# A hand-ordered head: two scan parts interleaved otherwise, states issued among the lag kernels, lag kernels in two column parts

## The chip, the cores and the metric

The kernel runs on one core of a Trainium2 chip. The metric is the device time of one execution in microseconds (us), the median of several runs. Before the change it is 1875.63 us (three runs, 1875.13 to 1880.0).

## The reference

One layer of a trunk: RMSNorm, an S5 mixer with a GLU, residual, RMSNorm, a gated convolutional FFN, residual, RMSNorm. There are 512 prompt tokens and 8 sample rows, D = 2048, D_FF = 5632; the S5 has 128 groups of 16 channels with 64 complex states each.

```python
def _s5_mixer(u, h_re, h_im, lam_re, lam_im, log_dt, b_re, b_im, c_re, c_im, d, w_glu):
    ...
    bu_re = jnp.einsum('gnp,btgp->btgn', bb_re, ug)
    bu_im = jnp.einsum('gnp,btgp->btgn', bb_im, ug)
    ...
    _, _, hs_re, hs_im = lax.associative_scan(combine, (a_re, a_im, bu_re, bu_im), axis=1)
    y = jnp.einsum('gpn,btgn->btgp', c_re, hs_re) - jnp.einsum('gpn,btgn->btgp', c_im, hs_im)
    y = y.reshape(bsz, t, D_MODEL) + d * uf
    z = jax.nn.gelu(y)
    out = z * jax.nn.sigmoid(z @ w_glu)
    return out, hs_re[:, -1], hs_im[:, -1]
...
    u = xn @ w_up ; gate = xn @ w_gate
    c = sum(full[:, j:j + t] * w_conv[j] for j in range(CONV_W)) + b_conv
    out = (jax.nn.gelu(c) * gate) @ w_down
```

## The kernel before

The program has two halves. The first, `s5_phase`, makes z, the input of the GLU. The second is dense matrix work on TensorE (L1182 for the GLU and the down projection, L1363 for the up and gate projections), each product of float32 taken as three products of high and low parts. It begins with the first matmul of L1182, which needs z of octet 0 and the first split weight.

In `s5_phase` the 128 groups are handled in eight octets (0 to 7). The prompt is cut into 64 chunks of 8 tokens. In each octet the work is: chunk inputs (C), then a scan over the chunks that carries the complex state, then from the state at each chunk's start its share in the outputs (F, L956), added on VectorE (O, L968) to the part that comes from inside the chunk (I, L827), transposed and passed through GELU (G, L977 and L980), and split into a high and a low part (Z). The part from inside the chunk is a matmul with a lag matrix; that one is made by `lag_kernel` (L, lines 887 to 893 on TensorE, a copy on ScalarE, a DMA to DRAM and one back). The tables for it are made by VectorE and GpSimd (tA, tB, tC).

The scan has two parts: "a" is octets 0 to 3, "b" octets 4 to 7, each with its own products (`sc0`, `sc1`) and sums (`wk0`, `wk1`). A chunk step of a part is three VectorE instructions, of which each needs the one before:

```python
            if k == 0:
                V.tensor_tensor(prod, v[:, :, None, :].to_broadcast([128, 2, 2, v.shape[2]]), tab, op=OP.mult)
            elif k == 1:
                V.tensor_tensor(w, vn, prod[:, 0], op=OP.add)
            else:
                V.tensor_tensor(vn, w, prod[:, 1], op=OP.add)
```

These are lines 219 (x), 221 (y) and 223 (z). A step is 128 partitions by 128 elements in x, by 64 in y and z.

What sets the order of work on every engine is a text, ORDER, written out by hand. `run` reads it from left to right. A token is a name and letters, as `a50x:D` (step 50 of the a part, instruction x, on VectorE): each name is a generator, and each letter lets it do its next stage. A, D, G stand for ScalarE, VectorE and GpSimd, Q for a DMA, a digit is a bank of PSUM, and `=w1s3` picks buffers. Each engine keeps the order in which its instructions are issued, and waits are made by data alone, so a token's place counts against the others of its engine.

At the start, ORDER holds the squares of the prompt rows (SQ), the row scales (RS: a matmul of L327, then the steps of `rsqrt_steps`, L104 to L115, on VectorE with one ScalarE root), the eight scaled rows (N, L146 or ScalarE), the transposes that make u (U, L345), and the products for the chunk inputs (mA, mB, mC on VectorE L674 and GpSimd L138).

Before, the two parts go step by step together from a14x on, the b part somewhat behind. The states F of octets 0 to 3 stand behind all eight lag kernels. F of octets 4 to 7 stands behind the b part's last instruction; then come G, Z and the split of the first weight (WT).

Of the kernel before, what the change touches and what calls it, by code (L numbers as in the profile page):

```python
# [59 lines left out]
a19x:D tC1.1:D =c0 cs2:G a19y:D tB1.1:D tB1.0:G SO1:Q a19z:D L0:A b5x:D a20x:D IB1:A b5y:D tC1.1:G a20y:D b5z:D a20z:D  # L60
b6x:D a21x:D b6y:D a21y:D b6z:D a21z:D =w0s6 tA2.0:G b7x:D a22x:D tB2.0:D SO0:Q =y1 SY0:1 a22y:D tB1.0:G b7y:D a22z:D
tB2.0:D a23x:D b7z:D =w1 tA2.1:G a23y:D b8x:D a23z:D tC2.1:D a24x:D tB2.1:G b8y:D =c0 cs4:D a24y:D b8z:D a24z:D b9x:D
a25x:D L1:0 b9y:D tC2.1:G SY0:A a25y:D tB2.1:D b9z:D a25z:D b10x:D =w1s2 tA3.0:G a26x:D tB3.0:D a26y:D b10y:D a26z:D
tC3.0:G b10z:D a27x:D b11x:D =m0 L0:Q a27y:D b11y:D a27z:D b11z:D SY1:3 a28x:D tB3.0:G IB2:A b12x:D tC3.0:D L1:A
# [25 lines left out]
I7:A I7:A GS3:A =y0 O4.0:D G3.0:0 F4.1:3 G3.0:A O4.1:D G3.1:2 G3.1:A =s2 Z3:A SF:G Z3:D F5.0:1 GS4:A =y1 O5.0:D G4.0:0  # L90
G4.0:A F5.1:3 O5.1:D G4.1:2 G4.1:A =s1 Z4:A Z4:D F6.0:1 GS5:A =y0 O6.0:D G5.0:0 G5.0:A F6.1:3 O6.1:D G5.1:2 G5.1:A =s0
Z5:A Z5:D F7.0:1 GS6:A =y1 O7.0:D G6.0:0 G6.0:A F7.1:3 O7.1:D SF:2 SF:A G6.1:1 G6.1:A =s7 Z6:D Z6:D GS7:A G7.0:0
G7.0:A G7.1:3 G7.1:A =s5 Z7:AD
# [1767 lines left out]
```

## Time and profile before

| | us |
|---|---|
| median of 3 runs | 1875.63 |
| profiled execution | 1877.71 |
| its span | 1875.9 |
| mean granted TensorE clock | 0.984 |
| TensorE busy | 1792.9 (96%) |
| VectorE busy | 1218.7 (65%) |
| ScalarE busy | 770.7 (41%) |
| GpSimd busy | 163.7 (9%) |

Engines in the rows: PE is TensorE's matmuls, PEld its weight loads, DVE VectorE, ACT ScalarE, POOL GpSimd. The shares are averages over two very different halves: the page's slices show VectorE and GpSimd full in the head and TensorE full behind it. A row of a timeline stands for one instruction or some of the same kind in a row (xN); its second number is from the first one's start to the last one's end. The end of a matmul is modelled.

### The profile page before, as it was taken

How to read it: one execution, taken by the hardware profiler on the slowest of the kernel's cores; microseconds unless marked ns; L12 is line 12 of the kernel's file. 1: busy time of each engine (PE TensorE's matmuls, PEld its weight loads, DVE VectorE, ACT ScalarE, POOL GpSimd, SP SyncE). 2: the span in 40 equal slices, each digit the busy share in tenths (PEclk: the TensorE clock that was granted, in tenths of full speed). 3: DMA queues.
4: the chain of work that ended last, by engine and by line, in shares of the span. 5: the costliest groups of instructions: out<-in, count | busy, mean ns of one | idle time of the engine just before them, and what ended most of it. 6: DMA issues, size and time to landing. Idle time of an engine off the chain costs nothing.

```text
span 1875.9 us, 36773 instructions
## 1 busy us (share of the span) xinstructions
PE 1792.9 (96%) x15962; PEld 1764.7 (94%) x15962; DVE 1218.7 (65%) x1812; ACT 770.7 (41%) x1103; POOL 163.7 (9%) x167
## 2 busy tenths in 40 slices
PE   3889999999699999999999999999999999999996
PEld 2778899999699999999999999999999999999996
DVE  8999633347887887887887887887733434343344
ACT  5763423344455454455445455544421212121223
POOL 4787201110000000000000000000000000000000
PEclk9989999999799999999999999999999999999998
DMA  7544254432434544443544534443663434333313
GB/s 148 118 136 145 72 161 141 136 125 102 146 124 147 190 136 169 169 147 124 185 165 144 194 125 147 152 133 124 221 214 94 144 98 138 103 124 118 113 68 92
DMA packets 217133, 259.43 MB, mean 138 GB/s; under 512 B 33859, under 2 KB 190491, under 8 KB 215867
## 3 DMA queue, kind: packets, MB, share of 16 engines
q1 hardware_dynamic: 213938, 252.17, 41.5%
q10 hardware_dynamic: 2842, 4.88, 0.9%
q8 instruction: 125, 2.05, 0.5%
q14 instruction: 36, 0.29, 0.1%
q0 software_dynamic: 192, 0.03, 0.0%
HBM read 226.11 MB, written 60.49 MB: 153 GB/s over the span
## 4 chain that ended last, share of the span: by engine, by line
PE 87%; DVE 6%; DMA 2%; ACT 2%; issue 1%; POOL 0%; SPq 0%; ACTq 0%; DVEq 0%; POOLq 0%
PE bank L1363 44%; PE bank L1182 35%; PE bank L1787 2%; PE py L956 1%; DMA x<-in_x_prompt_dram 1%; PE pv L698 1%; DVE m L138 1%; PE pm L683 1%; PE pk L893 1%; DVE op L1455 0%; DVE b L1442 0%; PE pu L345 0%; PE bank L1681 0%; DMA braw<-in_s_b_im_dram 0%; PE pt L977 0%
## 5 line engine op out<-in xcount | busy, mean ns | idle before, releaser
L1363 PE MATMUL bank<-op,w 128*128 128x260 f32 x5040 | 618.7, 284 | 9.0 <-DVE w L1337 5.2
L1363 PEld LDWEIGHTS bank<-op,w 128*128 128x128 f32 x5040 | 613.1, 189 | 10.6 <-DVE w L1337 5.7
L1182 PE MATMUL bank<-act,wh 128*128 128x260 f32 x2496 | 400.0, 282 | 0.0
L1182 PEld LDWEIGHTS bank<-act,wh 128*128 128x128 f32 x2496 | 341.3, 188 | 0.0
L1328 ACT ACTIVATE w<-raw 128x1024 fp32r<-128x1024 f32 x252 | 266.0, 1056 | 168.6 <-PE bank L1363 86.1
L1337 DVE TENSOR_TENSOR w<-raw,w 128x1024 fp32r<-128x1024 f32 x252 | 305.6, 1219 | 24.4 <-ACT w L1328 23.3
L1141 ACT ACTIVATE wh<-raw 128x2048 fp32r<-128x2048 f32 x61 | 116.8, 1916 | 464.5 <-PE bank L1182 462.7
L1363 PE MATMUL bank<-fz,w 128*128 128x260 f32 x2016 | 251.1, 284 | 5.1 <-DVE w L1337 4.8
L1363 PEld LDWEIGHTS bank<-fz,w 128*128 128x128 f32 x2016 | 246.7, 190 | 5.7 <-DVE w L1337 5.0
L1182 PE MATMUL bank<-act,wl 128*128 128x260 f32 x1248 | 250.9, 282 | 0.0
L1145 DVE TENSOR_TENSOR wl<-raw,wh 128x2048 fp32r<-128x2048 f32 x60 | 137.5, 2292 | 163.0 <-ACT wh L1141 163.0
L1182 PE MATMUL bank<-z,wh 128*128 128x260 f32 x1280 | 207.4, 284 | 3.2 <-DVE cps L1278 2.9
L1182 PEld LDWEIGHTS bank<-act,wl 128*128 128x128 f32 x1248 | 192.1, 188 | 0.0
L1182 PEld LDWEIGHTS bank<-z,wh 128*128 128x128 f32 x1280 | 176.4, 189 | 4.1 <-issue 3.3
L1182 PE MATMUL bank<-z,wl 128*128 128x260 f32 x640 | 129.0, 283 | 0.0
L1763 DVE TENSOR_TENSOR h<-h,bank 128x260 f32<-128x260 f32 x80 | 29.6, 421 | 130.9 <-PE bank L1182 130.9
L1763 DVE TENSOR_TENSOR uh<-uh,bank 128x260 f32<-128x260 f32 x80 | 29.6, 421 | 115.1 <-PE bank L1182 115.1
L1182 PEld LDWEIGHTS bank<-z,wl 128*128 128x128 f32 x640 | 98.9, 189 | 0.0
L1328 ACT ACTIVATE w<-s 128x1024 fp32r<-128x1024 f32 x42 | 44.6, 1062 | 74.8 <-PE bank L1363 73.1
L1586 DVE TENSOR_TENSOR us<-us,bank 128x260 f32<-128x260 f32 x21 | 8.9, 424 | 69.5 <-PE bank L1363 69.5
L1344 DVE TENSOR_TENSOR raw<-raw 128x1024 f32<-128x1024 f32 x42 | 51.4, 1225 | 1.4
L1341 DVE TENSOR_TENSOR raw<-raw,s 128x1024 f32<-128x1024 f32 x42 | 51.4, 1225 | 1.4
(351 smaller groups left out, 1811.3 us busy)
## 6 DMA issues: line engine op xcount, KB each, us to landing
raw<-in_ffn_w_down_dram SPq DMA_DIRECT2D x44, 1024.0 KB, 5.8
raw<-in_ffn_w_up_dram SPq DMA_DIRECT2D x42, 1024.0 KB, 5.1
raw<-in_ffn_w_gate_dram SPq DMA_DIRECT2D x42, 1024.0 KB, 6.8
raw<-in_s_w_glu_dram SPq DMA_DIRECT2D x16, 1024.0 KB, 6.2
a_dram<-cv SPq DMA_DIRECT2D x44, 260.0 KB, 2.1
src<-a_dram SPq DMA_DIRECT2D x11, 1040.0 KB, 8.1
x<-in_x_prompt_dram SPq DMA_DIRECT2D x16, 512.0 KB, 9.2
m<-kd SPq DMA_DIRECT2D x32, 256.0 KB, 4.5
```

Source lines behind the costliest of these rows:

```text
L138: engine[e].tensor_tensor(dst, a, b, op=op)
L683: PE.transpose(pm[:, e * 128:(e + 1) * 128], bps[o, eh][0][:, ri, e].rearrange("p q s -> p (q s)"), ident)
L1141: A.activation(hi, raw, AF.Copy)
L1145: engine[e].tensor_tensor(lo, raw, hi.bitcast(F32), op=OP.subtract)
L1182: PE.matmul(ps[hf][:, 0:HALF], w, x[:, hf * HALF:(hf + 1) * HALF], start=first and i < 2, stop=last and i >= 4)
L1328: A.activation(w[:, 0], u.q[name], AF.Copy)
L1337: V.tensor_tensor(w[:, 1], u.q[name], w[:, 0].bitcast(F32), op=OP.subtract)
L1341: V.tensor_tensor(u.q["A22"], u.q["A22"], u.q["S3"], op=OP.subtract)
L1344: V.tensor_tensor(u.q["A12"], u.q["A12"], u.q["S2"], op=OP.subtract)
L1363: PE.matmul(bank, w[:, a, kk], x[:, kk], start=name in BEGINS and kk + i == 0, stop=kk == 7 and i == 2, skip_group_check=True)
L1763: V.tensor_tensor(t, t, x, op=OP.add)
L1787: PE.matmul(ps, w[:, kk, ni * 128:(ni + 1) * 128], x[:, kk, c0:c1], start=kk + i == 0, stop=kk == 3 and i == 2)
```

## The change

The order text is rewritten in two stretches. In its head, the row scales RS come earlier, with no GpSimd operation issued next to them; scaled row N7 goes to GpSimd, N3 and N4 to ScalarE, the other five to VectorE (before: four each on ScalarE and VectorE); the clearing for the sample rows (SM) comes later. In the scan, from step 14 of the a part on, three a instructions stand for each b instruction, so the a part is ahead of the b part; F, O and G of octets 0 to 3 and the first high parts (Z) stand among the lag kernels and the rest of the b part; the low parts of octets 0 to 2 stand on VectorE behind the b part's end, where before two of them were on GpSimd.

`lag_kernel` issues its matmuls so that neighbours write the two halves of the output partitions (0 to 31, 32 to 63) in turn. Eight matmuls with the identity become two, with a summing matrix `stack` and a spread-out `dge`, which four ScalarE copies make; `stack` and `quarter` come from two more VectorE reductions. Four of the eight loads of x are issued on ScalarE's queue.

```diff
--- before.py
+++ after.py
@@ -25,10 +25,10 @@
...
-mB1.0:D mC1.0:G =b1p1 mA1.1:D AL:A RS:1 mC1.1:D mB1.0:G mP1.0.1:2 RS:D XU:D mB1.1:D RS:A XU:A RS:D mB1.1:G mP1.0.1:A
+=b1p1 mA1.1:D RS:D RS:A RS:D mB1.0:G N4:A N1:D N7:G DG0:A AL:A N5:D N2:D mP1.0.1:2 mP1.0.0:3 mC1.1:D N0:D N3:A XU:D
...
@@ -53,44 +53,44 @@
...
-a50x:D b32x:D tC6.1:G a50y:D b32y:D tB6.1:D a50z:D b32z:D YM:G a51x:D L6:1 b33x:D I3:A =c1 cs7:G a51y:D b33y:D a51z:D
...
+b13x:D a51x:D a51y:D a51z:D b13y:D tC5.0:G a52x:D a52y:D L4:3 =w0 tA5.1:D a52z:D b13z:D tB5.1:G a53x:D a53y:D a53z:D
...
@@ -189,6 +189,8 @@
         s5 = ctx.enter_context(tc.tile_pool(name="s5", bufs=1))
         vs = s5.tile([128, 73, 2, 64], F32, name="vs")
         dgm = s5.tile([128, 16, 16], F32, name="dgm")
+        stack = s5.tile([128, 32], F32, name="stack")
+        quarter = s5.tile([128, 4], F32, name="quarter")
         ysm = s5.tile([128, 2, 8, 8], F32, name="ysm")
         a1 = s5.tile([128, 2, 64], F32, name="a1")
         at3 = s5.tile([128, 3, 8, 64], F32, name="at3")
@@ -257,15 +259,15 @@
             nc.sync.dma_start(xs8, x_sample[:, 0, :])
             nc.sync.dma_start(xsr, dram(x_sample, 0, [[128, 128], [1, 128]]))
 
-            def load_x(i, where):
+            def load_x(i, where, second=nc.sync):
 
                 x = slot([128, 2, 1024], F32, "x", where)
                 for g2 in range(2):
-                    nc.sync.dma_start(x[g2 * 64:g2 * 64 + 64],
+                    (nc.sync, second)[g2].dma_start(x[g2 * 64:g2 * 64 + 64],
                                       dram(x_prompt, 2 * i * D + g2 * 1024, [[8 * D, 64], [D, 2], [1, 1024]]))
                 return x
 
-            xt = [load_x(i, i + 1) for i in range(4)]
+            xt = [load_x(i, i + 1, nc.scalar) for i in range(4)]
             for i, src_ in ((0, s5_d), (1, norm_mix)):
                 for g2 in range(2):
                     nc.gpsimd.dma_start(dld[:, i].rearrange("p (a g q) -> p a g q", a=4, g=2)[:, :, g2, :],
@@ -310,6 +312,8 @@
             dgc = s5t.tile([128, 2, 16], F32, name="dgc")
             mq = s5t.tile([128, 16], F32, name="mq")
             V.tensor_reduce(mq, ident.rearrange("p (a b) -> p b a", b=16), axis=AX.X, op=OP.add)
+            V.tensor_reduce(stack, ident.rearrange("p (a b) -> p b a", b=32), axis=AX.X, op=OP.add)
+            V.tensor_reduce(quarter, ident.rearrange("p (a b) -> p a b", b=32), axis=AX.X, op=OP.add)
             sel = s5t.tile([128, NB], F32, name="sel")
             V.tensor_reduce(sel, ident.rearrange("p (a b) -> p a b", b=16), axis=AX.X, op=OP.add)
 
@@ -840,6 +844,10 @@
         ysz = s5y.tile([128, 2, 8, 8], F32, name="ysz")
         for g2 in range(2):
             P.memset(bk[g2 * 64:g2 * 64 + 64, :, :, (1 - g2) * 16:(1 - g2) * 16 + 16], 0.0)
+
+        dge = s5y.tile([128, 16, 4, 16], F32, name="dge")
+        for e in range(4):
+            A.activation(dge[:, :, e], dgm, AF.Copy, scale=quarter[:, e:e + 1])
         m3s = {}
         css = {}
         w3 = {}
@@ -881,17 +889,23 @@
             kt = kts[o % 2]
             pk = pst("pk", (yield))
             m3 = m3s[o]
-            for e in range(8):
-                rows = slice((e // 4) * 32, (e // 4) * 32 + 32)
-                c0 = (e % 4) * 128
-                PE.matmul(pk[rows, c0:c0 + 16], ident[:, (e % 4) * 32:(e % 4) * 32 + 32], dgm[:, 2 * o + e // 4, :],
+            half = [slice(eh * 32, eh * 32 + 32) for eh in range(2)]
+            for eh in range(2):
+                PE.matmul(pk[half[eh]].rearrange("p (e k) -> p e k", e=4)[:, :, 0:16], stack, dge[:, 2 * o + eh],
                           start=True, stop=False)
+            for e4 in range(4):
+                c0 = e4 * 128
                 for ri in range(2):
-                    PE.matmul(pk[rows, c0:c0 + 16], bk[:, ri, e, :], ct[:, ri, o * 8 + e, :],
-                              start=False, stop=ri == 1)
+                    for eh in range(2):
+                        PE.matmul(pk[half[eh], c0:c0 + 16], bk[:, ri, eh * 4 + e4, :], ct[:, ri, o * 8 + eh * 4 + e4, :],
+                                  start=False, stop=e4 == 3 and ri == 1)
+            for e4 in range(4):
+                c0 = e4 * 128
                 for ri in range(2):
-                    PE.matmul(pk[rows, c0 + 16:c0 + 128], bk[:, ri, e, :],
-                              m3[:, ri, e, 0:7].rearrange("p k q -> p (k q)"), start=ri == 0, stop=ri == 1)
+                    for eh in range(2):
+                        PE.matmul(pk[half[eh], c0 + 16:c0 + 128], bk[:, ri, eh * 4 + e4, :],
+                                  m3[:, ri, eh * 4 + e4, 0:7].rearrange("p k q -> p (k q)"),
+                                  start=ri == 0, stop=ri == 1)
             yield
             copy("A", kt.rearrange("p l e q -> p e l q"),
                  pk[0:64].rearrange("p (e l q) -> p e l q", e=4, l=8))
```

VectorE, in the middle of the scan (sc_100 and wk_102 belong to the a part, sc_101 and wk_103 to the b part), before:

```order
L219 TENSOR_TENSOR sc_100<-vs,sc_100 128x128
L219 TENSOR_TENSOR sc_101<-vs,sc_101 128x128
L221 TENSOR_TENSOR wk_102<-vs,sc_100 128x64
L221 TENSOR_TENSOR wk_103<-vs,sc_101 128x64
L223 TENSOR_TENSOR vs<-wk_102,sc_100 128x2x32
L223 TENSOR_TENSOR vs<-wk_103,sc_101 128x2x32
```

The same place after (now sc_102 and wk_104 belong to the a part, sc_103 and wk_105 to the b part, and the lines are 221, 223 and 225):

```order
L221 TENSOR_TENSOR sc_103<-vs,sc_103 128x128
L221 TENSOR_TENSOR sc_102<-vs,sc_102 128x128
L223 TENSOR_TENSOR wk_104<-vs,sc_102 128x64
L225 TENSOR_TENSOR vs<-wk_104,sc_102 128x2x32
L223 TENSOR_TENSOR wk_105<-vs,sc_103 128x64
L221 TENSOR_TENSOR sc_102<-vs,sc_102 128x128
L223 TENSOR_TENSOR wk_104<-vs,sc_102 128x64
L225 TENSOR_TENSOR vs<-wk_104,sc_102 128x2x32
L225 TENSOR_TENSOR vs<-wk_105,sc_103 128x2x32
```

Before, an instruction of one part always stands between two that depend on each other; now x, y and z of the a part follow each other directly, with one b instruction after each z.

TensorE, where the states of octet 0 come (m_0 is octet 0's table, m_7 octet 7's), before:

```order
L887 MATMUL pk<-dgm,ident 32x16
L890 MATMUL pk<-ct,bk 32x16 x2
L893 MATMUL pk<-m_7_2375,bk 32x112 x2
L956 MATMUL py<-m_0_1411,vs 64x128 x32
L956 MATMUL py<-m_1_1487,vs 64x128 x16
L977 MATMUL pt<-ident,ys 128x128 x4
```

The same place after (lag kernels are lines 894 to 906, the intra part 831, the states 970, the transposes 991):

```order
L831 MATMUL py_2263<-m_2173,uz 64x128 x8
L831 MATMUL py_2272<-m_2173,uz 64x128 x8
L970 MATMUL py<-m_0_1420,vs 64x128 x32
L894 MATMUL pk<-dge,stack 32x4x16 x2
L900 MATMUL pk<-ct,bk 32x16 x16
L906 MATMUL pk<-m_6_2178,bk 32x112 x16
L991 MATMUL pt<-ident,ys 128x128 x4
L970 MATMUL py<-m_1_1496,vs 64x128 x16
```

The states of octet 0 stood behind the lag kernel of octet 7; now they stand ahead of that of octet 6.

## Rows read from the trace of the kernel before

**Rows 1.** The page: span.
```profile
span 1875.9 us, 36773 instructions
```

**Rows 2.** Stages: PE, PEld, DVE, ACT, POOL busy (count), PEclk, DMA share, GB/s.
```profile
90.25:181.10 90.85, 79.28 (x1361) 71.83 (x1360) 89.84 (x377) 46.34 (x87) 76.60 (x68) 0.89 0.48 145
181.10:205.83 24.73, 24.73 (x372) 22.64 (x372) 17.80 (x63) 8.83 (x15) 4.81 (x2) 0.97 0.34 94
...
231.49:1875.90 1644.41, 1609.43 (x13325) 1603.93 (x13325) 1017.49 (x1177) 644.72 (x883) 23.57 (x34) 0.99 0.42 140
```

**Rows 3.** DVE timeline, a part alone: start, length, instruction, count, [idle before].
```profile
104.41 0.30 DVE L219 TENSOR_TENSOR sc<-vs,sc 128x128 f32<-128x128 f32 x1
104.74 0.22 DVE L221 TENSOR_TENSOR wk<-vs,sc 128x64 f32<-128x64 f32 x1
104.99 0.22 DVE L223 TENSOR_TENSOR vs<-wk,sc 128x64 f32<-128x64 f32 x1
105.25 0.30 DVE L219 TENSOR_TENSOR sc<-vs,sc 128x128 f32<-128x128 f32 x1
```

**Rows 4.** DVE timeline, both parts interleaved.
```profile
176.51 0.48 DVE L219 TENSOR_TENSOR sc<-vs,sc 128x128 f32<-128x128 f32 x2
176.91 0.34 DVE L221 TENSOR_TENSOR wk<-vs,sc 128x64 f32<-128x64 f32 x2
177.17 0.34 DVE L223 TENSOR_TENSOR vs<-wk,sc 128x64 f32<-128x64 f32 x2
177.43 0.48 DVE L219 TENSOR_TENSOR sc<-vs,sc 128x128 f32<-128x128 f32 x2
```

**Rows 5.** DVE timeline, b part alone: two x in turn.
```profile
198.67 0.30 DVE L219 TENSOR_TENSOR sc<-vs,sc 128x128 f32<-128x128 f32 x1
...
199.51 0.30 DVE L219 TENSOR_TENSOR sc<-vs,sc 128x128 f32<-128x128 f32 x1
```

**Rows 6.** DVE timeline, last rows of the a part and the b part.
```profile
180.85 0.34 DVE L223 TENSOR_TENSOR vs<-wk,sc 128x64 f32<-128x64 f32 x2
...
205.62 0.21 DVE L223 TENSOR_TENSOR vs<-wk,sc 128x64 f32<-128x64 f32 x1
```

**Rows 7.** DVE waits from 181.1 to 206: total, times, longest us.
```profile
DVE ys L968 <- PE py L956: 5.3, 4, 3.4
```

**Rows 8.** TensorE in a window: PE busy (count), PEclk, DMA share, GB/s.
```profile
176.00:178.00 2.00, 1.83 (x14) 0.50 0.32 80
```

**Rows 9.** PE timeline of the tail.
```profile
207.31 2.08 PE L956 MATMUL py<-m,vs 64*64 64x128 f32 x32
209.32 0.66 PE L977 MATMUL pt<-ident,ys 128*128 128x128 f32 x4
209.91 2.07 PE L956 MATMUL py<-m,vs 64*64 64x128 f32 x32
...
214.28 2.08 PE L956 MATMUL py<-m,vs 64*64 64x128 f32 x32 [1.72 <-DVE ys L968]
...
231.49 0.74 PE L1182 MATMUL bank<-z,wh 128*128 128x260 f32 x4 [0.25 <-ACT uz L980]
```

**Rows 10.** Head: timelines of DVE, PE and POOL, and one window as in rows 2.
```profile
35.00 0.17 DVE L104 TENSOR_SCALAR rq<-prs 128x8 f32<-128x8 f32 x1 [2.86 <-PE prs L327]
...
35.97 2.44 DVE L111 TENSOR_TENSOR rq<-rq,rs 128x8 f32<-128x8 f32 x2
...
39.13 0.64 DVE L115 TENSOR_TENSOR rs<-rs,rq 128x8 f32<-128x8 f32 x1
...
47.13 2.03 DVE L146 TENSOR_SCALAR vs<-x,rs 128x1024 f32<-128x1024 f32 x1
...
49.31 2.79 PE L345 MATMUL pu<-ident,vs 128*128 128x128 f32 x12 [1.22 <-DVE vs L146]
...
35.90 2.48 POOL L138 TENSOR_TENSOR bp<-bb,bp 128x512 f32<-128x512 f32 x2 [2.97 <-DVE bp L674]
...
30.00:32.00 2.00, 0.00 (x0) 0.00 (x0) 2.00 (x4) 0.01 (x1) 1.57 (x2) 1.00 1.07 229
```

More of the change, by code (lines that the diff above doesn't have):

```diff
@@ L27 @@
 ORDER = """
-=s5 SM:A SQ1:A SQ0:A SQ2:A SQ3:A SQ4:A =s6 XR1:Q SQ5:A AK:G SQ6:A =b0p0s7 mA1.0:D DG0:0 AK:G mC1.0:D DG0:A SQ7:A
-mB1.0:D mC1.0:G =b1p1 mA1.1:D AL:A RS:1 mC1.1:D mB1.0:G mP1.0.1:2 RS:D XU:D mB1.1:D RS:A XU:A RS:D mB1.1:G mP1.0.1:A
-mP1.0.0:3 mQ1.0:A XU:D N4:A mC1.1:G mP1.1.0:0 N1:D N5:A N2:D XU:1 AK:G mP1.1.1:2 mP1.0.0:D mP1.1.0:A =s3 CL0:Q AK:G
-N3:A mP1.1.1:D AM:G XU:D N0:D N7:A =s2 R1.0:0 =b0p2s1 mA2.0:D DG:G R1.0:A R1.2:3 R1.3:2 N6:D R1.1:1 ST:A R1.2:D AM:G
+SQ1:A SQ0:A SQ2:A SQ3:A SQ4:A =s6 XR1:Q SQ5:A AK:G SQ6:A =b0p0s7 mA1.0:D DG0:0 AK:G mC1.0:D SQ7:A RS:1 mB1.0:D mC1.0:G
+=b1p1 mA1.1:D RS:D RS:A RS:D mB1.0:G N4:A N1:D N7:G DG0:A AL:A N5:D N2:D mP1.0.1:2 mP1.0.0:3 mC1.1:D N0:D N3:A XU:D
+XU:A mP1.0.1:A mP1.0.0:D mB1.1:D mC1.1:G mB1.1:G mQ1.0:A mP1.1.0:0 XU:D XU:1 mP1.1.1:2 mP1.1.0:A =s3 CL0:Q AK:G
+mP1.1.1:D AK:G AM:G XU:D =s5 SM:A =s2 R1.0:0 =b0p2s1 mA2.0:D DG:G R1.0:A R1.2:3 R1.3:2 N6:D R1.1:1 ST:A R1.2:D AM:G
 U3.0:0 =b1p0s4 mA0.0:D R1.3:A U7.1:3 R1.1:A U3.0:D U0.1:2 AC:A LC0.1:1 U7.1:D AC:A U3.1:0 U0.1:A mB0.0:D U1.1:3 U3.1:A
@@ L60 @@
[L60 to L64, printed above, removed]
@@ L90 @@
[L90 to L93, printed above, removed]
+tB0.0:G C7.1.1:1 R0.3:A a13x:D R2.0:A R2.1:2 a13y:D C7.1.1:A a13z:D R2.3:3 tC0.1:G a14x:D SB:A a14y:D R2.2:0 a14z:D
@@ new lines @@
+b1x:D a15x:D W0:Q a15y:D tB0.0:D tB0.1:G a15z:D R2.1:A tC0.1:D R2.2:A tC0.0:G b1y:D SP6:D R2.3:A a16x:D SP7:D =w1s3
+tA1.0:G a16y:D a16z:D =y0 SO0:1 SH:A b1z:D a17x:D a17y:D W2:Q a17z:D tC1.0:G b2x:D =y1 SO1:2 a18x:D a18y:D a18z:D
+b2y:D a19x:D a19y:D a19z:D tC0.0:G b2z:D SO1:A0 a20x:D a20y:D tC1.0:D SO0:A3 a20z:D SO1:A =w0 tA1.1:G tB1.1:D L0:0
+SO0:A b3x:D tC1.1:D =c0 cs2:G a21x:D tB1.1:D tB1.0:G SO1:Q a21y:D L0:A a21z:D b3y:D IB1:A a22x:D tC1.1:G a22y:D a22z:D
+b3z:D a23x:D a23y:D a23z:D b4x:D a24x:D a24y:D =w0s6 tA2.0:G a24z:D b4y:D tB2.0:D SO0:Q =y1 SY0:1 a25x:D tB1.0:G
@@ new lines @@
+a25y:D a25z:D tB2.0:D b4z:D a26x:D =w1 tA2.1:G a26y:D a26z:D b5x:D tC2.1:D a27x:D tB2.1:G a27y:D =c0 cs4:D a27z:D
+b5y:D a28x:D a28y:D a28z:D L1:2 b5z:D tC2.1:G SY0:A a29x:D tB2.1:D a29y:D a29z:D b6x:D =w1s2 tA3.0:G a30x:D tB3.0:D
+a30y:D a30z:D b6y:D tC3.0:G a31x:D a31y:D a31z:D =m0 L0:Q b6z:D a32x:D a32y:D a32z:D SY1:3 b7x:D tB3.0:G IB2:A a33x:D
+tC3.0:D L1:A a33y:D a33z:D tC2.0:G b7y:D a34x:D =w1 tA3.1:D a34y:D =c1 cs5:D tC3.1:G a34z:D tC2.0:D b7z:D tB3.1:D L2:0
+tC3.1:G SY1:A a35x:D a35y:D MTB:A a35z:D b8x:D a36x:D a36y:D a36z:D tB3.1:G b8y:D a37x:D a37y:D a37z:D b8z:D a38x:D
@@ new lines @@
+a38y:D =w0s1 tA4.0:G a38z:D b9x:D a39x:D =m1 L1:Q a39y:D a39z:D b9y:D a40x:D SZ:1 a40y:D =w1 tA4.1:G a40z:D IB3:A
+tC4.0:D SZ:A b9z:D L2:A tC4.1:D tB4.1:G a41x:D tC4.0:D a41y:D I0:2 I0:3 L3:0 a41z:D tC4.1:G b10x:D tB4.1:D a42x:D
+a42y:D tB4.0:G a42z:D b10y:D a43x:D a43y:D a43z:D b10z:D I0:A a44x:D a44y:D =c0 cs6:G =w1s0 tA5.0:D I0:A L3:A tB5.0:G
+a44z:D b11x:D a45x:D a45y:D a45z:D b11y:D a46x:D tC5.0:G a46y:D =m0 L2:Q a46z:D b11z:D a47x:D a47y:D I1:1 I1:2 a47z:D
+b12x:D IB4:A tB5.0:G a48x:D a48y:D a48z:D b12y:D a49x:D a49y:D I1:A a49z:D b12z:D tB4.0:G I1:A a50x:D a50y:D a50z:D
@@ new lines @@
+b13x:D a51x:D a51y:D a51z:D b13y:D tC5.0:G a52x:D a52y:D L4:3 =w0 tA5.1:D a52z:D b13z:D tB5.1:G a53x:D a53y:D a53z:D
+b14x:D a54x:D a54y:D a54z:D L4:A b14y:D tC5.1:G a55x:D IB5:A a55y:D tB5.1:D I2:0 I2:1 a55z:D =m1 L3:Q =w1s7 tA6.0:G
+b14z:D a56x:D tC5.1:D I2:A a56y:D a56z:D L5:2 b15x:D I2:A tB6.0:G tC6.0:D a57x:D a57y:D a57z:D b15y:D tC6.0:G a58x:D
+a58y:D a58z:D b15z:D IB6:A a59x:D a59y:D a59z:D tB6.0:G b16x:D L5:A a60x:D a60y:D a60z:D b16y:D a61x:D a61y:D a61z:D
+=w0 tA6.1:G b16z:D a62x:D a62y:D a62z:D b17x:D a63x:D a63y:D tC6.1:D tB6.1:G a63z:D I3:3 I3:0 F0.0:1 b17y:D =m0 L4:Q
@@ new lines @@
+b17z:D b18x:D b18y:D tC6.1:G b18z:D b19x:D tB6.1:D b19y:D F0.1:2 b19z:D YM:G b20x:D L6:3 b20y:D I3:A =c1 cs7:G =y0
+O0.0:D b20z:D b21x:D b21y:D I3:A b21z:D =w1s5 tA7.0:G b22x:D =m1 L5:Q b22y:D b22z:D GS0:A b23x:D b23y:D b23z:D O0.1:D
+b24x:D b24y:D tB7.0:G L6:A b24z:D b25x:D IB7:A b25y:D b25z:D G0.0:0 b26x:D b26y:D b26z:D tC7.0:G G0.0:A F1.0:1 b27x:D
+b27y:D b27z:D b28x:D G0.1:2 b28y:D b28z:D G0.1:A b29x:D b29y:D tB7.0:G b29z:D b30x:D F1.1:3 tC7.0:D I4:0 I4:1 =s4 Z0:A
+b30y:D =y1 O1.0:D b30z:D =w0 tA7.1:G b31x:D b31y:D b31z:D b32x:D GS1:A tB7.1:D tC7.1:G b32y:D O1.1:D b32z:D I4:A
@@ new lines @@
+b33x:D b33y:D b33z:D I4:A b34x:D b34y:D =m0 L6:Q b34z:D tB7.1:G G1.0:2 b35x:D b35y:D G1.0:A b35z:D F2.0:3 b36x:D
+b36y:D b36z:D I5:0 I5:1 G1.1:2 b37x:D b37y:D tC7.1:G b37z:D G1.1:A L7:3 b38x:D b38y:D b38z:D F2.1:0 b39x:D b39y:D I5:A
+b39z:D =s3 Z1:A b40x:D =y0 O2.0:D b40y:D I5:A b40z:D b41x:D b41y:D b41z:D L7:A b42x:D =m1 L7:Q E2:G b42y:D GS2:A
+b42z:D b43x:D O2.1:D b43y:D b43z:D b44x:D b44y:D b44z:D b45x:D b45y:D G2.0:1 b45z:D b46x:D G2.0:A b46y:D F3.0:2 I6:3
+I6:0 b46z:D b47x:D b47y:D b47z:D G2.1:1 I6:A I6:A b48x:D b48y:D G2.1:A b48z:D b49x:D b49y:D b49z:D F3.1:2 b50x:D
@@ new lines @@
+b50y:D b50z:D =s6 Z2:A =y1 O3.0:D b51x:D b51y:D b51z:D b52x:D b52y:D b52z:D b53x:D GS3:A b53y:D b53z:D O3.1:D I7:3
+I7:0 b54x:D b54y:D b54z:D b55x:D b55y:D I7:A I7:A b55z:D b56x:D G3.0:1 b56y:D b56z:D G3.0:A b57x:D b57y:D b57z:D
+b58x:D b58y:D G3.1:2 b58z:D b59x:D G3.1:A b59y:D b59z:D b60x:D b60y:D b60z:D b61x:D b61y:D =s2 Z3:A b61z:D b62x:D
+b62y:D b62z:D b63x:D b63y:D b63z:D Z0:D F4.0:3 WT:A F4.1:0 =y0 O4.0:D Z1:D WT:G F5.0:1 GS4:A O4.1:D Z2:D G4.0:2 F5.1:3
+G4.0:A =y1 O5.0:D G4.1:0 G4.1:A F6.0:1 GS5:A O5.1:D =s1 Z4:A Z4:D G5.0:2 G5.0:A F6.1:3 =y0 O6.0:D G5.1:0 G5.1:A Z3:D
@@ L94 @@
+F7.0:1 GS6:A O6.1:D =s0 Z5:A Z5:D G6.0:2 G6.0:A F7.1:3 =y1 O7.0:D G6.1:0 SF:G SF:1 SF:A G6.1:A O7.1:D =s7 Z6:D GS7:A
+Z6:D G7.0:2 G7.0:A G7.1:3 G7.1:A =s5 Z7:AD
 """
```

28 lines of the change are left out of this document (removed).

## The prediction, made before the result was known

> **What bounds the kernel now.** I read the page first, then a table by stages, then the rows at the seams of the stages. The span is 1875.9 us [rows 1] and the profiled execution took 1877.71 us. The stage table [rows 2] shows two kernels in one. From 231.49 us to the end TensorE is busy 1609.43 of 1644.41 us: everything there stands behind the dense matmuls, and whatever starts them later by so much ends the program later by so much. The 231.49 us ahead of that are the head, and the change touches the head alone. So the whole question is when the first matmul of L1182 starts.
>
> What sets that time? From 90.25 to 181.10 us VectorE is busy 89.84 of 90.85 us with TensorE at 79.28 [rows 2]. VectorE carries the scan: 63 steps, in two parts (octets 0 to 3, "a"; octets 4 to 7, "b"), each step three dependent instructions x, y, z. The a part ends with the row at 180.85 (end 181.19), the b part with the row at 205.62 (end 205.83) [rows 6]. Behind the b part comes the tail on TensorE: the states' matmuls of octet 4 start at 207.31 and L1182 at 231.49, 24.18 us later, with 1.72 and 0.25 us idle in it [rows 9]. The end of the b part plus a tail sets the end of the head.
>
> **What a scan step costs.** Rows 3 show the a part with nothing between: x at 104.41, y 0.33 later, z 0.25 later, next x 0.26 later: 0.84 us a step. Rows 5 show the b part by itself: 198.67 to 199.51, again 0.84. Rows 4 show both parts interleaved, x x y y z z: 176.51 to 177.43, 0.92 us for two steps (0.40 for the two x, 0.26 for two y, 0.26 for two z). So the second step of a pair costs 0.08 us and a step by itself costs 0.84. An instruction that depends on the one right ahead of it waits some 0.25 to 0.33 us from start to start, and an independent one fits into that wait almost for nothing.
>
> **The change, part by part.**
> 1. *Scan order.* Before, the b part has done 44 of its 63 steps when the a part ends. By step counts: 19 a steps alone (15.96), 44 pairs (40.48) and 19 b steps alone (15.96), 72.40 us of scan. Now a whole a step runs for each single b instruction. That makes 14 a steps alone (11.76), 49 a steps with one b instruction in each, and 49 instructions are 16.3 b steps, so 46.7 b steps are left alone (39.20). For the mixed step I take 0.33 (x to y) + 0.255 (y to z, nothing between) + the stretch from z over the b instruction to the next x: 0.26 where that is a y or z [rows 4], 0.33 where it is an x (between 0.26 and the 0.40 of two x): 0.868 on the mean, 42.53 for 49. Sum 93.49, **+21.1 us**. The a part ends only 2 us earlier, and the b part has 23 us more behind it. Bounds: with 0.40 after each b instruction the mixed step is 0.985 and the sum +26.8; below, nothing at all if the order is free on VectorE (rival A). I take the middle, since the rows for both spacings stand in the trace.
> 2. *States among the lag kernels.* Before, the additions of the outputs wait 5.3 us for TensorE in four waits, the longest 3.4 [rows 7], with b instructions queued behind. TensorE came late there: it still had a lag kernel to do, after a stretch at a granted clock of 0.50, its lower level of 1.2 GHz (176 to 178 us, [rows 8]). Now the states of octet 0 are issued right behind the a part and their addition stands some 15 scan instructions later, so most of this goes: **-5.3**, and +1.5 for new waits (bounds 0 and the old 5.3; I stay near the 1.9 us that the three short waits make). The scan instructions behind a waiting addition are what such a wait delays.
> 3. *Lag kernel in two column parts.* Eight identity matmuls become two, and neighbouring matmuls go to different parts. TensorE is not the bound while the scan runs; VectorE is. I cost it at nothing for the end; if TensorE were to pace the b stretch, the price is in rival C. The four new ScalarE copies are hidden by ScalarE's idle half (46.34 of 90.85 us busy, [rows 2]); the two new reductions stand ahead of VectorE's 2.86 us wait for the row scales at 35.00 [rows 10].
> 4. *Head of the order.* The row-scale chain's last four instructions run from 35.97 to 39.77 us, the first two of them in 2.44 us beside a GpSimd operation of 2.48 us at 35.90, where one on a tile of the same size takes 0.17 at 35.00 [rows 10]. Now no GpSimd operation stands beside the chain; four instructions at some 0.2 us each (an estimate from that 0.17) make 0.8 us in place of 3.8: **-3.0**, carried to the scan's start at 90.25 as VectorE is nearly full. Bounds 0 (the first transposes at 49.31 wait for the last scaled row of VectorE, which then waits for something else) and -6 (GpSimd takes a scaled row off too; one of 128x1024 at 47.13 takes VectorE 2.03 beside GpSimd). The second queue for the x loads brings nothing: the DMA share is 1.07 at 229 GB/s at 30 to 32 us [rows 10].
> 5. *Tail.* Octet 4's states now start right behind the last scan instruction, not behind the intra matmuls: 0.15 us behind it (as 49.16 to 49.31, [rows 10]). Two transposes of octet 3 (0.59 each, 209.32 to 209.91, [rows 9]) are done ahead: 24.18 - 1.18 = 23.0. Three low parts moved to VectorE lie beside TensorE's work there; I leave the 1.97 us of idle time as it is (bounds 0 and twice that).
>
> Sum: the b part ends at 205.83 - 3.0 + 21.1 - 5.3 + 1.5 = 220.1; states of octet 4 at 220.3; L1182 at 243.2 against 231.49: +11.7 us. On the profiled execution that is 1877.71 + 11.7 = 1889.4; on the median of the runs, 1875.63, which lies 2.1 us under it, **1887.3 us**. With the bounds of head (3 each way), waits and idle taken in part, 1882 to 1893 for this case.
>
> **Rivals.**
> A. *The order costs VectorE nothing.* If an instruction takes its time wherever it stands, term 1 vanishes: the b part ends near 199.0, L1182 starts at 222.1, -9.4 us, 1866.2. For it: both kernels issue the same 378 scan instructions, and VectorE is recorded busy all through. Against it: 0.84 alone and 0.92 for two [rows 3 to 5]. It decides if a lone step falls under 0.6 us.
> The Trainium skill, "VectorE: DVE Perf Modes", § "The DRAIN you can't avoid", says that the next operation can't start until the pipe has emptied, whether or not a semaphore stands between, which would price a step alike in any order and give rival A. The rows above disagree: six instructions in 0.92 us stand against three in 0.84.
> B. *Everything else at its good end.* The order costs 21.1, but the head gives 6, no addition waits and the tail has no idle time: 3.0 + 1.5 + 2.0 better, +5.2 us, 1880.8: inside what I call no change. For it: the head's 2.44 us rows are slowed indeed. Against: three good ends at once.
> C. *TensorE slow in the b stretch.* With 46.7 lone steps TensorE has states, transposes and the last intra and lag matmuls spread over some 45 us, and in the kernel before it was granted 0.50 from 176 to 178 us though it was busy 1.83 of these 2.00 us [rows 8]. One such 6 us stretch costs an addition another 3.4 us of waiting [rows 7], one at the start of the tail 3 us: +6.4, 1893.7. For it: more idle time per us than now (between 181 and 206 us it was busy all along, 24.73 of 24.73, [rows 2]). Against: the waits are late enough to be missed.
>
> **Chances.** Forecast 0.57, A 0.08, B 0.13, C 0.22. 0.3% (5.6 us) is about what can be told from no change. A is faster, B the same, the forecast and C slower: 0.08, 0.13, 0.79. The range takes in B, C and the forecast with their spreads: 1878 to 1897.
>
> **What would show it.** In the profile after: a lone b stretch of some 39 us at 0.84 a step behind the a part's end near 176 us; that stretch's VectorE waits on TensorE under 2 us; the row-scale chain's last four instructions in under 1.5 us; L1182 at about 243. I am wrong if the mixed step costs much less or more than 0.87, if lone steps run at under 0.6, or if L1182 starts before 237.

## The result and the profile after

The changed kernel takes 1893.05 us (median of 4 runs, 1892.59 to 1893.94) against 1875.38 for the kernel before. The ratio is 1.0091, 95% interval 1.0079 to 1.0103; by that ratio it is 17 us slower (15 to 19 by the interval). Forecast were 1887.3 (+11.7) and a range of 1878 to 1897. The profiled execution took 1892.6 us.

The stages of the changed kernel (TensorE busy, its weight loads, VectorE, ScalarE, GpSimd, each with its count; then granted clock, DMA share, GB/s), cut at the first scan instruction, the end of the a part, the end of the b part and the first dense matmul, to be held against [rows 2]:

```profile
92.89:178.39 85.50, 61.76 (x1136) 53.87 (x1136) 81.08 (x289) 44.33 (x84) 63.45 (x57) 0.84 0.46 133
178.39:224.90 46.51, 33.85 (x543) 30.29 (x541) 40.00 (x153) 18.54 (x30) 13.80 (x12) 0.92 0.33 94
...
224.90:246.05 21.15, 21.07 (x288) 19.23 (x284) 14.40 (x16) 6.33 (x14) 3.61 (x2) 0.94 0.17 51
246.05:1890.80 1644.75, 1609.51 (x13327) 1603.73 (x13325) 1018.53 (x1178) 645.48 (x885) 23.16 (x34) 0.99 0.42 140
```

The last row is the dense part: 1644.75 us, and 1644.41 before. Nothing changed there, it only starts later: 246.05 against 231.49. All of the loss is in the head, and it falls into three stretches:

| stretch | before | after | difference | forecast |
|---|---|---|---|---|
| start to the first scan instruction | 90.25 | 92.89 | +2.64 | -3.0 |
| first scan instruction to the b part's end | 115.58 | 132.01 | +16.4 | +17.3 |
| b part's end to the first dense matmul | 25.66 | 21.15 | -4.5 | -2.5 |
| sum | 231.49 | 246.05 | +14.6 | +11.8 |

The forecast's own sum carries +11.7, a tenth less than its terms. The middle stretch is the scan, and it is what the order did. VectorE's timeline (start, length, instruction) shows the mixed stretch, three a steps with a b instruction in each:

```profile
148.17 0.49 DVE L221 TENSOR_TENSOR sc<-vs,sc 128x128 f32<-128x128 f32 x2
148.69 0.22 DVE L223 TENSOR_TENSOR wk<-vs,sc 128x64 f32<-128x64 f32 x1
148.94 0.22 DVE L225 TENSOR_TENSOR vs<-wk,sc 128x64 f32<-128x64 f32 x1
149.08 0.21 DVE L223 TENSOR_TENSOR wk<-vs,sc 128x64 f32<-128x64 f32 x1
149.21 0.29 DVE L221 TENSOR_TENSOR sc<-vs,sc 128x128 f32<-128x128 f32 x1
...
150.77 0.49 DVE L221 TENSOR_TENSOR sc<-vs,sc 128x128 f32<-128x128 f32 x2
```

From 148.17 to 150.77 are three a steps and one b step: 2.60 us, 0.867 for each a step (forecast 0.868). The b part by itself, behind the a part:

```profile
207.20 0.29 DVE L221 TENSOR_TENSOR sc<-vs,sc 128x128 f32<-128x128 f32 x1
207.53 0.22 DVE L223 TENSOR_TENSOR wk<-vs,sc 128x64 f32<-128x64 f32 x1
207.79 0.22 DVE L225 TENSOR_TENSOR vs<-wk,sc 128x64 f32<-128x64 f32 x1
208.04 0.29 DVE L221 TENSOR_TENSOR sc<-vs,sc 128x128 f32<-128x128 f32 x1
```

It takes 0.84 us a step, as in [rows 5], and the stretch behind the a part now lasts 46.51 us where it was 24.64. The additions of the outputs wait for TensorE once:

```profile
DVE ys L982 <- PE py L970: 2.1, 1, 2.1
```

That answers to [rows 7]: 5.3 us in four waits have become 2.1 in one. The head shows two things that the forecast did not have: VectorE's first instruction waits for a small load until 7.28 us (4.58 before), and work has piled up behind the row scales. VectorE's timeline:

```profile
7.28 0.22 DVE L278 COPY lds<-ldt 64x128 f32<-64x128 f32 x1 [7.28 <-DMA ldt<-in_s_log_dt_dram]
...
34.64 0.16 DVE L104 TENSOR_SCALAR rq<-prs 128x8 f32<-128x8 f32 x1
...
36.56 0.17 DVE L115 TENSOR_TENSOR rs<-rs,rq 128x8 f32<-128x8 f32 x1
36.77 3.91 DVE L146 TENSOR_SCALAR vs<-x,rs 128x1024 f32<-128x1024 f32 x3
```

GpSimd's timeline behind them, and TensorE's:

```profile
36.91 5.64 POOL L146 TENSOR_SCALAR vs<-x,rs 128x1024 f32<-128x1024 f32 x1 [0.81 <-issue]
42.44 2.07 POOL L138 TENSOR_TENSOR bp<-bb,bp 128x512 f32<-128x512 f32 x1
```

```profile
46.06 1.11 PE L687 MATMUL pm<-ident,bp 128*128 128x128 f32 x4 [8.79 <-POOL bp L138]
48.81 0.59 PE L495 MATMUL prb<-dg,one 8*128 8x8 f32 x2 [1.63 <-DVE dg L493]
...
53.54 1.47 PE L349 MATMUL pu<-ident,vs 128*128 128x128 f32 x12
```

The row scales end at 36.7 us, not at 39.8: the 3.0 us were won there. Then the scaled row N7 keeps GpSimd for 5.64 us, and its next product starts at 42.44. TensorE waits 8.79 us, until 46.06, for the product after that one. That product does not wait for GpSimd alone. It needs a product of VectorE first, and VectorE makes that one behind four scaled rows (three in 3.91 us from 36.77, one in 2.40 us from 41.11). VectorE's rows, then that product on GpSimd:

```profile
41.11 2.40 DVE L146 TENSOR_SCALAR vs<-x,rs 128x1024 f32<-128x1024 f32 x1
...
44.00 0.67 DVE L678 TENSOR_TENSOR bp<-bt,qt 128x512 f32<-128x512 f32 x1
```

```profile
44.75 1.26 POOL L138 TENSOR_TENSOR bp<-bb,bp 128x512 f32<-128x512 f32 x1 [0.24 <-DVE rx L108]
```

The transposes that make u stand behind all of this in TensorE's order: they start at 53.54 (before 49.31, [rows 10]).

### The profile page after: what moved, and what is told of

Same layout as the page of the kernel before. It is cut to its first block, busy times and chain, and to the rows that moved or that the text cites. A ratio compares the mean times of both kernels' runs of the same rounds, so it can differ in the third digit from the quotient of the medians.

```text
span 1890.8 us, 36590 instructions
## 1 busy us (share of the span) xinstructions
PE 1781.5 (94%) x15866; PEld 1752.4 (93%) x15866; DVE 1235.3 (65%) x1817; ACT 768.3 (41%) x1105; POOL 163.5 (9%) x166
## 4 chain that ended last, share of the span: by engine, by line
PE 85%; DVE 10%; ACT 2%; issue 2%; DMA 1%; SPq 0%; ACTq 0%; DVEq 0%
PE bank L1377 44%; PE bank L1196 34%; PE bank L1801 2%; DVE sc L221 1%; PE py L970 1%; DVE wk L223 1%; DVE vs L225 1%; DVE m L138 1%; DVE bp L678 1%; DMA braw<-in_s_b_re_dram 1%; DVE op L1469 0%; DVE b L1456 0%; PE bank L1695 0%; DMA x<-in_x_prompt_dram 0%; PE pu L349 0%
```

## The experiments

All changed kernels below are held against the changed kernel's 1893.05 us, unless the text says otherwise; ratios are to the kernel before, measured on the same chip in alternation. Some of the profiled runs lie up to 2.7 us off the median of their kernel, so what is said of a median rests on the timed runs, and the trace serves for where the time stands.

**The dependence (free_b).** The b part's instructions read older data, and so none needs the result of the one ahead.

```diff
-            v, vn, w = vs[:, c, :, parts[i]], vs[:, c + 1, :, parts[i]], wk[i][:, c % 2]
+            v, vn, w = vs[:, c - i, :, parts[i]], vs[:, c + 1, :, parts[i]], wk[i][:, c % 2]
+            w2 = wk[i][:, (c + (i if c > 1 else 0)) % 2]
+            other = scn[0][:, 1]
...
-                V.tensor_tensor(w, vn, prod[:, 0], op=OP.add)
+                V.tensor_tensor(w, vn, other[:, 0], op=OP.add)
-                V.tensor_tensor(vn, w, prod[:, 1], op=OP.add)
+                V.tensor_tensor(vn, w2, (other if i else prod)[:, 1], op=OP.add)
```

> The changed kernel, in which the b part's x, y and z read older tables, so that no b instruction needs the one right ahead of it (the b states, and so the outputs, are other numbers; the count, shapes and engines of all instructions are the same). Theory (a lone step costs 0.84 us since each instruction waits for the one ahead): b steps fall from 0.84 to under 0.6 us in the stretch after the a part; 46.7 steps by 0.25 to 0.38 us make it 12 to 18 us shorter, unless TensorE then bounds it: 1875 to 1882 us. Rival (instructions of this size cost 0.25 to 0.33 us each wherever they stand, or the tables in PSUM cost it): steps stay at 0.84 us and the time at 1891 to 1895 us.

Measured: 1889.76 us (ratio 1.0074, 1.0059 to 1.0090). VectorE's timeline in the b stretch:

```profile
189.51 0.29 DVE L223 TENSOR_TENSOR sc<-vs,sc 128x128 f32<-128x128 f32 x1
189.71 0.22 DVE L225 TENSOR_TENSOR wk<-vs,sc 128x64 f32<-128x64 f32 x1
189.96 0.22 DVE L227 TENSOR_TENSOR vs<-wk,sc 128x64 f32<-128x64 f32 x1
190.09 0.29 DVE L223 TENSOR_TENSOR sc<-vs,sc 128x128 f32<-128x128 f32 x1
```

The same instructions now take 0.58 us a step: x to y 0.20 in place of 0.33, z to x 0.13 in place of 0.25. From y to z it is still 0.25: z no longer reads what y writes, but it still overwrites the row of `vs` that y reads. So the order of what depends on what costs VectorE time, and rival A's mechanism is refuted. The time, however, fell by 3 us and not by 12 to 18: the expectation missed it. From octet 0's states to octet 4's it now takes 38.0 us (180.38 to 218.34) in place of 47.1 (177.15 to 224.21). But octet 0's states start 3.2 us later. In the mixed stretch the b part's y and z now read the product that the a part's next x overwrites, and that x starts 0.25 us behind them, where it was 0.13 (149.08 to 149.21 above):

```profile
150.18 0.21 DVE L225 TENSOR_TENSOR wk<-vs,sc 128x64 f32<-128x64 f32 x1
150.43 0.30 DVE L223 TENSOR_TENSOR sc<-vs,sc 128x128 f32<-128x128 f32 x1
```

That comes twice in three a steps, 0.24 us; over the 16 groups of three it is some 4 us (an estimate). And the tail has new idle time, 2.14 us, and a slow row of states, 3.62 us for 2.1. The dense part starts at 242.46, 3.6 earlier.

**The scan's order undone (old_scan).** The order text from a14x on is that of before, all else the changed kernel's.

```diff
-tB0.0:G C7.1.1:1 R0.3:A a13x:D R2.0:A R2.1:2 a13y:D C7.1.1:A a13z:D R2.3:3 tC0.1:G a14x:D SB:A a14y:D R2.2:0 a14z:D
+tB0.0:G C7.1.1:1 R0.3:A a13x:D R2.0:A R2.1:2 a13y:D C7.1.1:A a13z:D R2.3:3 tC0.1:G a14x:D SB:A b1x:D R2.2:0 a14y:D
...
```

> The changed kernel (its head, its loads, its lag kernel in two column parts) with the scan's order of before. Theory (the scan's order carries the loss): the dense matmuls start near 234 us, 12 us earlier than in the changed kernel, since only the head's 2.6 us are left: 1878 to 1882 us. Rival (the lag kernel's new form or the states among the lag kernels carry it): over 1887 us.

Measured: 1879.13 us (ratio 1.0019, 1.0009 to 1.0029). The order from a14x on, with all that it moves, is worth 13.9 us, and what is left of the loss is 3.2 to the 1875.92 of before in the same runs.

**How many b instructions in an a step (two_b, three_b).** Two, and three, b instructions in each a step in place of one; what stands between the scan instructions stays in its place.

```diff
-a44z:D b11x:D a45x:D a45y:D a45z:D b11y:D a46x:D tC5.0:G a46y:D =m0 L2:Q a46z:D b11z:D a47x:D a47y:D I1:1 I1:2 a47z:D
...
+b22y:D a47x:D b22z:D a47y:D I1:1 I1:2 a47z:D b23x:D IB4:A tB5.0:G a48x:D b23y:D a48y:D a48z:D b23z:D a49x:D b24x:D
...
```

> The changed kernel with two b instructions in each a step (before: about three, the change: one), so that 30 b steps in place of 46.7 are left behind the a part; everything else keeps its place between the scan instructions. Theory (a lone dependent step costs 0.84 us, a mixed one about 0.92): the scan takes 82 us in place of 93.5, the dense matmuls start 8 to 12 us earlier than in the changed kernel (234 to 238 us): 1881 to 1885 us. Rival (the scan's order is not it, but the states among the lag kernels): within 3 us of the changed kernel, over 1889.

> The same with three b instructions in each a step: 13.7 b steps left. If VectorE alone set the end, this would be 13 us faster still than two per step (1868 to 1872). If TensorE's own work behind the a part's end (some 36 us of states, transposes, intra and lag matmuls ahead of octet 4's states) takes over as the bound, nothing more is won over two per step: 1879 to 1885 us, with VectorE waiting for TensorE in the b stretch for more than 8 us. I expect the second.

Measured: 1887.37 us (1.0062, 1.0048 to 1.0076) and 1885.64 us (1.0052, 1.0037 to 1.0067). Two of them give back 5.7 us, less than expected; three give 7.4. So the interleaving by itself gives back only a bit over half of the 13.9 us. Three_b's stretch from octet 0's states to the b part's end, and VectorE's waits for TensorE from 170 to 230 us:

```profile
182.36:216.20 33.84, 32.88 (x558) 29.79 (x560) 19.36 (x61) 14.70 (x27) 12.10 (x11) 1.00 0.49 134
```

```profile
DVE ys L981 <- PE py L969: 9.9, 5, 5.4
```

TensorE is busy 32.88 of 33.84 us, VectorE 19.36, and 9.2 us of VectorE's waits for TensorE lie in this stretch. The bound has gone over to TensorE, as the second half of the expectation had it, if not quite in its time (1885 at most). In old_scan the same stretch is this:

```profile
184.41:205.86 21.45, 21.45 (x320) 19.55 (x322) 18.45 (x68) 8.24 (x14) 4.81 (x2) 1.00 0.38 105
```

558 records of matmuls against 320. The new order puts more lag and intra matmuls behind octet 0's states, and these 11 us of TensorE are the second limit. The 6.5 us from 1885.64 to 1879.13 us are then what the places of the other work cost, with the scan interleaved in both; which part of that work carries them was not tried apart.

**The lag kernel by itself (lag_only).** The kernel before with the new `lag_kernel` and its tables alone.

> The order text and the loads of before with the lag kernel in two column parts alone (and its tables). Theory A (TensorE is the bound between the a part's end and the tail in the kernel before, busy 24.7 of 24.7 us, so a shorter lag kernel of octet 7 brings the states forward): the first addition's wait of 3.4 us falls under 1 us and the end comes 2 to 4 us earlier than before: 1872 to 1874 us. Theory B (off the path, as the prediction costed it): 1875 to 1877 us, no difference from before.

Measured: 1876.0 us (ratio 0.9999, 0.9991 to 1.0008): no difference, within some 1.6 us. Theory A fell. TensorE does an octet in little more than half the time: the changed kernel's rows run from 180.97 to 183.32, 2.35 us for 34 matmuls, where an octet of 40 took 4.35 with the lag kernel of before (177.56 to 181.91 in before_again, the next run; the granted clock is 1.00 in both).

```profile
180.97 0.31 PE L894 MATMUL pk<-dge,stack 128*32 128x64 f32 x4
181.11 0.66 PE L900 MATMUL pk<-ct,bk 128*32 128x16 f32 x32
181.61 1.71 PE L906 MATMUL pk<-m,bk 128*32 128x112 f32 x32
```

But only the last octet's kernel lies where TensorE is waited for, and with it shorter the states of octet 0 wait for the scan itself (0.80 us in lag_only). The 3 us that lag_only's trace shows (dense matmuls from 228.29) are mostly the luck of the trace of before, as the next run shows.

**The kernel before once more (before_again).** No edit.

> The kernel before, once more, for its trace: the profiled run of before stood 2.1 us over the median, while lag_only's stood 1.4 us under its own. If that profile drew a late head, the first dense matmul starts now at 228 to 230 us (not 231.5) with the first addition's wait at 1 to 3 us; if not, at 231 to 232 with 3.4 us again.

Measured: 1876.77 us in a single run, the scan's start at 89.27, the first dense matmul at 229.02, the longest wait of an addition 1.9 us. So the trace that the forecast was made from had drawn a late first dense matmul, by 2.5 us. The dense part took 1.6 us longer in this run.

**The head (old_head, n7_act, one_queue, chain_early).** Old_head has the order of before up to the scaled rows and all x loads on SyncE. N7_act and one_queue change one token and one argument, chain_early a part of a line:

```diff
-... RS:D RS:A RS:D mB1.0:G N4:A N1:D N7:G DG0:A ...
+... RS:D RS:A RS:D mB1.0:G N4:A N1:D N7:A DG0:A ...
```

```diff
-            xt = [load_x(i, i + 1, nc.scalar) for i in range(4)]
+            xt = [load_x(i, i + 1) for i in range(4)]
```

```diff
-RS:D RS:A RS:D mB1.0:G N4:A N1:D N7:G DG0:A AL:A N5:D N2:D mP1.0.1:2 mP1.0.0:3 mC1.1:D N0:D N3:A XU:D XU:A ...
+RS:D RS:A RS:D mC1.1:D XU:D XU:A mB1.0:G N4:A N1:D mB1.1:D mC1.1:G mB1.1:G XU:D XU:1 N7:A DG0:A AL:A N5:D N2:D ...
```

> The changed kernel with the order of before up to the scaled rows and all x loads on SyncE's queue; scan and lag kernel are the new ones. Theory (the new head costs 2.6 us): the scan starts at 90.3 us as before, and all behind it is 2 to 3 us earlier: 1890 to 1891 us. Rival (the new head is no loss, other runs of the same head vary by as much): 1893 us, scan start at 92 or later.

> The changed kernel with the scaled row N7 on ScalarE in place of GpSimd, nothing else. Theory (GpSimd's 5.64 us for N7 holds up its next products, which TensorE waited 8.79 us for): the scan starts at 87 to 90 us, the time falls by 3 to 6: 1887 to 1890 us. Rival (VectorE's five scaled rows and the moved chain of the sample rows cost it): scan start at 92 to 94 us, 1892 to 1894 us.

> The changed kernel with all x loads on SyncE's queue. Theory (half the x loads on ScalarE's queue are issued ahead of the small loads on SyncE's and delay them, log_dt from 4.6 to 7.3 us, so VectorE's table work starts 2.7 us later): that work starts at 4.6 us again, but the row scales wait for the squares at 34 to 35 us either way: the scan's start moves by less than 1.5 us, 1891.5 to 1894 us. Rival (the whole head stands behind that work): 2.5 to 3 us faster, 1890 to 1890.6 us.

> The changed kernel with N7 on ScalarE and, between the row scales and the scaled rows, the two products and the sample rows' chain that the new head had put behind them on VectorE. Theory (with N7 off GpSimd the head lost its remaining 2 us because TensorE's transposes for u stand behind the products' and the sample rows' matmuls, whose VectorE operations had moved behind four scaled rows): the transposes of u start at 48 to 50 us (51.7 with N7 alone moved, 53.5 in the changed kernel), the scan at 88 to 90 us, the time 1888.5 to 1890.5 us. Rival (the scaled rows themselves are now later by as much): u at 51 us or later, scan start at 90.5 or later, 1891 to 1892 us.

| kernel | u starts | scan starts | median us | ratio (interval) |
|---|---|---|---|---|
| changed | 53.54 | 92.89 | 1893.05 | 1.0091 (1.0079 to 1.0103) |
| one_queue | 53.27 | 92.66 | 1892.61 | 1.0090 (1.0076 to 1.0103) |
| n7_act | 51.72 | 91.10 | 1891.45 | 1.0082 (1.0066 to 1.0098) |
| chain_early | 49.19 | 89.20 | 1890.72 | 1.0080 (1.0063 to 1.0097) |
| old_head | 49.06 | 88.86 | 1891.47 | 1.0079 (1.0063 to 1.0095) |

The traces put it in order: N7 away from GpSimd starts u 1.8 us earlier, and the products and the sample rows' chain ahead of the scaled rows another 2.5. In the medians this is 1.6 and 0.7 us, within the intervals of each other; the starts are shown by one trace each (with the head of before, u starts at 49.06 to 49.55 in five traces). On time, old_head, n7_act and chain_early all came out above what was expected of them.

What N7 on GpSimd cost shows on VectorE. Its first four scaled rows took 6.31 us beside GpSimd's N7, and without it, in n7_act, 4.24:

```profile
37.16 3.08 DVE L145 TENSOR_SCALAR vs<-x,rs 128x1024 f32<-128x1024 f32 x3
...
40.66 1.16 DVE L145 TENSOR_SCALAR vs<-x,rs 128x1024 f32<-128x1024 f32 x1
```

That the new head is slower is clearer in the scan's start than in the medians: in five traces with the head order and the loads of before (before, before_again, lag_only, wt_dve, old_head) it lies at 88.86 to 90.25 us, in five with the new ones (the changed kernel, old_scan, two_b, three_b, free_b) at 92.64 to 93.36. The means are 3.4 us apart. One_queue: VectorE's work starts at 4.57 us again (in the changed kernel log_dt, issued at 2.23 us, landed 2.7 us late; ScalarE's queue had issued a load of x at 1.49), and nothing comes of it, since the row scales wait for the squares:

```profile
35.16 0.17 DVE L104 TENSOR_SCALAR rq<-prs 128x8 f32<-128x8 f32 x1 [3.13 <-PE prs L331]
```

In the changed kernel that wait was 0: the late start had used up the cover.

**Better than both? (wt_dve, best1).** Wt_dve is lag_only with the low part of the first weight on VectorE behind octet 4's outputs; best1 is wt_dve with the row scales ahead as in the change, but no scaled row on GpSimd.

```diff
-... I7:2 F4.0:1 WT:G Z2:D I7:A I7:A GS3:A =y0 O4.0:D G3.0:0 F4.1:3 G3.0:A O4.1:D G3.1:2
+... I7:2 F4.0:1 Z2:D I7:A I7:A GS3:A =y0 O4.0:D G3.0:0 F4.1:3 G3.0:A O4.1:D WT:D G3.1:2
```

> lag_only with the low part of the first weight (4.54 us on GpSimd) on VectorE behind octet 4's outputs. Theory (VectorE's low part of octet 2 takes 4.72 us in the tail only because GpSimd works beside it): that operation falls to 1.2 to 1.5 us, TensorE's 1.72 us of idle time at octet 5's states goes, the tail is 1 to 2 us shorter: 1874 to 1875.5 us. Rival: the idle time moves to another wait of the tail, 1875.5 to 1877.

> wt_dve with the row scales ahead as in the changed kernel, but four scaled rows each on ScalarE and VectorE and the sample rows' chain where it was before. Theory (the early row scales are worth 3 us, and N7 on GpSimd with the late sample chain, which stands ahead of the transposes on TensorE, threw them away): the transposes that make u start at 45.5 to 47.5 us (before 49.3), the scan 1 to 3 us earlier than 90.2, and the time is 1 to 3 us under wt_dve's: 1871 to 1874. Rival (something else holds the head, such as the other GpSimd products): scan start at 90 us or later, same time as wt_dve.

Measured: 1873.65 us (ratio 0.9988, 0.9979 to 0.9998) and 1873.64 (0.9989, 0.9980 to 0.9998). Wt_dve is about 2 us faster than the kernel before, and TensorE's idle 1.72 us at octet 5's states is gone from its trace; its interval overlaps lag_only's, so the edit's own share is shown by the trace alone. Best1 adds nothing, the rival: its row scales end at 36.2, but the GpSimd products that slowed them now stand beside the next chain of small instructions, and u starts at 48.72:

```profile
35.41 0.37 DVE L110 TENSOR_TENSOR rq<-rq,rs 128x8 f32<-128x8 f32 x2
...
38.57 2.49 DVE L110 TENSOR_TENSOR rx<-rx 8x1 f32<-8x1 f32 x2
```

```profile
38.55 2.50 POOL L137 TENSOR_TENSOR bp<-bb,bp 128x512 f32<-128x512 f32 x2 [5.14 <-DVE rx L107]
```

## Why the prediction was right, and where not

1. *Scan order, +21.1.* Right in mechanism and nearly in size. A mixed step took 0.867 us (0.868 forecast), a lone step 0.84, and with the two wait terms the stretch came to +16.4 against +17.3. Within it the a part took 3.3 us less than counted and the b part 2.4 more, partly since three table products (at 179.86, 190.62 and 193.24 us) stand behind the a part's end now.
2. *Waits of the additions, -5.3 and +1.5.* One of 2.1 us is left: -3.2 in place of -3.8.
3. *Lag kernel, nothing.* Right: lag_only shows no difference.
4. *Head, -3.0.* This is the step that failed; it measured +2.6, outside its bounds of 0 and -6. The row-scale chain did get its 3 us: its last four instructions took 1.42 us (35.31 to 36.73) in place of 3.80, and they started 0.7 earlier. What failed is that they were "carried to the scan's start". The bound "-6, GpSimd takes a scaled row off too" was taken as a gain at its end, though no row showed what such a row costs on GpSimd (5.64 us, and 2.1 more for VectorE's own rows beside it), and a bound above 0 was missing. What stands behind the scaled rows on VectorE and on TensorE was not followed. N7_act and chain_early together bring the scan's start back to 89.20, the level of the head of before, and no earlier; nor does best1, which has the early row scales without N7 on GpSimd (89.66). So the 3 us of the chain reached the scan's start in no run. The 5.6 us between -3.0 and +2.6 are more than the whole difference between forecast and result in the traces (+11.7 against +14.6); that the tail gave 2 us back is luck, as far as the forecast goes.
5. *Tail, -2.5.* It gave -4.5. The idle time of 1.97 us that I kept is gone, and octet 4's states start at 224.21, 0.7 us ahead of the b part's end: they read the state at each chunk's start and need only the step before the last. Against this the first three groups of states ran in 7.1 us where 6.0 is usual, at a granted clock of 0.77, after TensorE had waited 5.52 us for the scan:

```profile
224.21 7.15 PE L970 MATMUL py<-m,vs 64*64 64x128 f32 x96 [5.52 <-DVE vs L225]
```

```profile
224.21:231.29 7.08, 7.08 (x96) 0.77 0.41 122
```

Of the rivals, A's mechanism was refuted by free_b, and its price was wrong too: in three_b, with the interleaving restored and the other work where the change put it, TensorE holds the end at 237.9, not at 222.1. The section of the Trainium skill that the prediction names with A ("VectorE: DVE Perf Modes", § "The DRAIN you can't avoid") does not give A when it is read whole, for it adds that "A next op that is not held starts earlier". That goes with free_b, where instructions that did not depend on the one ahead started 0.13 and 0.20 us behind it. C came in part: 1.1 us at the tail's start and one wait of 2.1. B did not come.

The loss is 17 us by the ratio and 14.6 in the two traces: the trace of before had a late draw (against before_again, with its first dense matmul at 229.02, the dense part starts 17.0 us later).

## What to carry to other kernels

Two dependent chains on one engine should run beside each other for as long as both last: a step of the second chain cost 0.08 us beside the first and 0.84 alone, so running one ahead only moves its steps to where they cost ten times as much. Before moving an operation to an idle engine, look up what that engine takes for it and what slows beside it, and follow the work behind it up to the engine that waits: N7 took 5.64 us on GpSimd and made VectorE's rows beside it 2.1 us longer, and the 3 us that the early row scales had won never reached the scan. A bound that is lifted shows the next: ask where the second engine's work will stand.
